# A hybrid convolution and attention block on one core: three pieces of work moved in the step order

## The chip, the cores and the metric

The kernel runs on one core of a Trainium2 chip. What counts is the device time of one execution in microseconds (us), the median of several runs. The core has five engines with a queue each: TensorE (PE: matmuls, PEld: its weight loads), VectorE (DVE), ScalarE (ACT), GpSimd (POOL) and SyncE (SP), whose queue here only issues DMAs. An engine executes its queue in order; semaphores tie the queues together.

## The reference

One layer of a diffusion block, 1024 tokens, width 1024, all in float32:

```python
h = rms_norm(x, g_pre) * (1 + sc) + sh              # sc, sh from silu(c) @ w_mod
ua, gate_a, q, k, v, gate_b, gm = split(h @ w_in)   # context tokens give k_c, v_c only
q, k = rope(rms_norm(q)), rope(rms_norm(k))         # 16 query heads, 4 key heads, 64 wide
o = softmax(q @ k_all.T / 8) @ v_all                # 1024 + 256 keys
y_attn = (o * silu(gate_b)) @ w_attn_out
a, g = split(ua); y = a * sigmoid(g)
y = depthwise_conv(y, 31 taps) + conv_b
y_conv = (silu(layer_norm(y)) * silu(gate_a)) @ w_conv_out
out = (sigmoid(ga) * y_conv + sigmoid(gb) * y_attn) @ w_out
x + gt * rms_norm(out, g_post)
```

## The kernel before, in words

Precision. A float32 operand of the large matmuls is split into a high and a low part, and three matmuls (`mm3`) replace one: high by high, low by high, high by low. Splitting a weight tile is a load (`wraw`), a cast on ACT (`whi`) and a subtraction on POOL or DVE (`wlo`).

Channels are laid on partitions, in 8 blocks of 128; tokens run along the free dimension.

**Fill steps.** All projections that no one waits for at once (convolution input, gates, sigmoids) stand in one generator, `fill`. One fill step is one `mm3` of 128x512, and 16 of them make one weight block for all tokens. There are NF = 720 of these steps ahead of the convolution's output projection. `filler(n)` issues n of them between the pieces of other work, so that PE always has something to do.

**Taps.** The depthwise convolution is 31 steps on DVE for each of the 8 channel blocks: `first` (on ACT) starts the sum, then 30 `tap`s add one shifted product of 128x1024. They stand in a list, `taps`; `pump(n)` issues the next n. Block 0 accumulates in SBUF (`acc`), blocks 1 to 7 start in PSUM in a tile `pconv` of the pool `conv`; the last tap of a block writes to SBUF. `in_psum` holds whether new sums start in PSUM, and which block is there. When `in_psum[0]` is false, the next tap moves the sum to SBUF, and the next block starts there. `last` adds the block to `ysum` on POOL and stores it to DRAM (`accD`).

**Order of the program.** (1) Preamble: modulation, normalisation and the context's keys, and then `rope_tables()` and the split weights of the first of four head groups (`group_w(0)`), both with fill steps between. (2) A loop of 4 x 4 projections: `qkv_mm` (48 matmuls of 128x384, `po`), then `per` fill steps, between which stand taps, and the steps of a generator `bg` that prepares the next group's weights. (3) The remaining fill steps up to number 464, with a tap for each two of them. Here the keys and the first rows for attention are loaded from DRAM (`load_group`, `max_load`). (4) The switch: the PSUM pools `conv` and `m`/`o` are given up, and the pools for attention opened in their place (`s` for scores, three buffers `m`). `max_piece(0, i)` finds row maxima of window 0: a matmul to `pm`, and a maximum over it on DVE (`mx`). (5) Attention: 16 windows of 20 steps (`i` in the loop over `2 * NS`). A step issues one score (two matmuls to `ps`, an exponential on ACT), one `max_piece` of the next window and one fill step; every tenth step issues 20 matmuls `po` for the values. Generators in `late` do other work at numbered steps, and their `yield n` says after how many steps they go on: `conv_rest` issues the remaining taps, the layer norm's mean (`ln_mean`: two matmuls of `ones` with `ysum`), its variance (`ln_var`), and the normalised and gated result (`z_prep`). (6) Output projections.

**What sets the order on each engine.** Up to the end of stage 2, PE, DVE, ACT and POOL keep program order. From there PE alone keeps it. A list scheduler orders the other engines, with a higher priority for what stands under `urgent()` (the maxima and exponentials, and the steps of `late`, these after the newest maximum).

In the rows below and in the trace, all operations have the line L51 (a helper), and are told apart by their tiles. A tap in PSUM is `pconv<-y,cw,pconv`, one that moves the sum is `acc<-y,cw,pconv`, and one in SBUF is `acc<-y,cw,acc`.

Of the kernel before, what the change touches and what calls it, by code (L numbers as in the profile page):

```python
# [35 lines left out]
def block_kernel(ctx: ExitStack, tc: tile.TileContext, x, cx, cc, wmod, bmodT, bmodg, vecs, gpost,  # L36
# [30 lines left out]
    def tl(tag, shape, bufs, dtype=F32, pool="sb"):  # L67
        return pools[pool].tile(list(shape), dtype, tag=tag, bufs=bufs, name=nm(tag))
# [6 lines left out]
    def closed(p):  # L75
        p.__exit__(None, None, None)
# [572 lines left out]
    def pump(n):  # L649
        for _ in range(min(n, len(taps))):  # L650
            taps.pop(0)()
# [26 lines left out]
    in_psum = [True, 0]  # L678
# [213 lines left out]
    ln = {}  # L892
# [60 lines left out]
    def z_prep():  # L953
        a, g = {}, {}

        def load(j):
            a[j] = tl("y4", (P, T), 3)
            SP.dma_start(out=a[j][:], in_=accD[j][:])
        load(0)
        for j in range(KD):  # L960
            g = tl("y4", (P, T), 3)
            SP.dma_start(out=g[:], in_=gaD[j][:])
            yield 3
            if j + 1 < KD:
                load(j + 1)
            yield 3
            for tok in HALVES:
                V.tensor_tensor(out=a[j][:, tok], in0=a[j][:, tok], in1=ln["r"][:, tok], op=ALU.mult)
                yield 1
            yield 1  # L970
            th = tl("ysum", (P, T), 1)
            S.activation(th[:], a[j][:], AF.Tanh, scale=lngh[:, j:j + 1], bias=lnbh[:, j:j + 1])
            S.activation(a[j][:], a[j][:], AF.Identity, scale=lng[:, j:j + 1], bias=lnb[:, j:j + 1])
            G.tensor_tensor(out=a[j][:], in0=a[j][:], in1=g[:], op=ALU.mult)
            yield 3
            for tok in HALVES:
                V.scalar_tensor_tensor(out=a[j][:, tok], in0=th[:, tok], scalar=1.0, in1=a[j][:, tok], op0=ALU.add,
                                       op1=ALU.mult)
                yield 1
            SP.dma_start(out=gaD[j][:], in_=a[j][:])  # L980
            yield 1

    zt = []

    def z_split(hf):
        a = {}

        def load(j):
            a[j] = tl("y4", (P, 512), 3)
            SP.dma_start(out=a[j][:], in_=gaD[j][:, hf * 512:hf * 512 + 512])  # L990
        if hf == 0:
            zt.extend(halves(KD))
        load(0)
        load(1)
        yield 3
        for j in range(KD):
            if j + 2 < KD:
                load(j + 2)
            split(zt[j][0][hf][:], zt[j][1][hf][:], a[j][:])
            yield 1 + j % 2  # L1000
# [137 lines left out]
    def filler(n):  # L1138
        done[0] += n
        return run(fill, n)  # L1140
# [3 lines left out]
    def work(n):  # L1144

        for _ in range(n):
            filler(1)
            owed[0] = min(owed[0] + RATE, 3.0)
            while owed[0] >= 1:
                pump(1)  # L1150
                owed[0] -= 1

    RATE = 0.25
    ck = ctx_kv()
    for d in ctx_h():
        work(d)
    RATE = 0.45
    for d in ck:
        work(d)
    RATE = 0.2  # L1160
    closed(stp)
    app = opened("A")
    wgp = opened("wg")
    for d in rope_tables():
        work(d)
    ones_rows()
    for d in group_w(0):
        work(d)
    prev = None
    bg = iter(())  # L1170
    per = (NF - done[0] - NB - 72) // 16
    for g in range(NG):
        for q in range(4):
            mm = qkv_mm(g, q)
            next(mm)
            if prev:
                qkv_rope(*prev)
            else:
                pump(3)
            next(mm)  # L1180
            next(mm)
            pump(3)
            next(mm)
            due = 0 if q == 3 else -1
            if q == 2 and g < NG - 1:
                bg = group_w(g + 1)
                next(bg)
            for i in range(per):
                filler(1)
                if i % 5 in (1, 3):  # L1190
                    pump(1)
                if i == 2 and prev:
                    qkv_tr(*prev)
                if i == 4:
                    z = next(mm)
                if i == 9:
                    z = qkv_scale(g, q, z)
                if i == due:
                    d = next(bg, None)
                    due = i + d if d else -1  # L1200
            if q == 3:
                run(bg)
            prev = (g, q, z)
    RATE = 0.5
    work(2)
    qkv_rope(*prev)
# [13 lines left out]
    while NF - done[0] > NB + 16:  # L1220
        filler(2)
        pump(1)
    in_psum[0] = False
    while in_psum[1]:
        pump(1)
    unshare(2)
    share({"m": 3, "o": 1})
    share({"s": 2})
    for i in range(20):
        filler(1)  # L1230
        max_piece(0, i)
        if i % 2:
            with tc.issue_after(crit[0].ins):
                pump(1)
    max_cols(0)
# [20 lines left out]
    def conv_rest():  # L1256
        while taps:
            pump(1)
            yield 2
        yield 3  # L1260
        ln_mean()
        yield 6
        yield from ln_var()
        yield from z_prep()
    later(1, conv_rest())
    for i in range(2 * NS):
# [25 lines left out]
        for g in late.pop(i, []):  # L1292
            with tc.issue_after(crit[0].ins), urgent():
                d = next(g, None)
# [81 lines left out]
```

## Time and profile before

| what | value |
|---|---|
| median of 3 runs (lowest to highest) | 1450.83 us (1448.73 to 1453.27) |
| the profiled execution: its time, its span | 1451.74 us, 1449.7 us |
| PE busy | 1384.7 us, 96% of the span |
| DVE busy | 998.6 us, 69% |
| stage 1 (to the first `po` of the projections) | 0 to 150.7 us |
| stages 2 and 3 (to the first `pm` of window 0) | to 560.9 us |
| stage 4 (to the first wait of a score) | to 586.6 us |
| stage 5 | to about 1222 us |
| stage 6 | to 1449.7 us |

The span runs from the first instruction to the last; 2.0 us of the execution lie outside it. In a row of the timeline stand the start, the duration, the engine, and `output<-inputs`; what follows in brackets is the time the engine idled before, and what ended it. In a row of windows stand, for each engine, its busy time and number of instructions, then the granted TensorE clock (1.00 is full), the DMA share and GB/s.

### The profile page before, as it was taken

Reading aid. Unit: us, or ns where it says so; the run is one execution under the profiler, and the core shown is the slowest. Engines: PE = TensorE matmul, PEld = TensorE weight load, DVE = VectorE, ACT = ScalarE, POOL = GpSimd, SP = SyncE. Lnnn points to the kernel's source line nnn. Section 1 sums busy time; section 2 is a strip of 40 time slices with the busy share of each in tenths; the row PEclk is TensorE's granted clock in tenths of the full one; section 3 lists DMA queues with packets and bytes.
Section 4 is the critical chain, followed back from the end, with each engine's and each line's share of the span. In section 5 each row is a group of like instructions: output and inputs, shape, how many; then the busy total and the mean of one; then the engine's idle time right before and its main releaser. Section 6 shows DMA issues by size and latency. Waiting matters only on the chain.

```text
span 1449.7 us, 18678 instructions
## 1 busy us (share of the span) xinstructions
PE 1384.7 (96%) x6584; PEld 1049.8 (72%) x6584; DVE 998.6 (69%) x1289; ACT 551.4 (38%) x1359; POOL 528.2 (36%) x359
## 2 busy tenths in 40 slices
PE   5988999999999998679999999999999999999998
PEld 3777989889898887446666666666666666676886
DVE  3477988888978897957776767777686653263522
ACT  5442344344443422225444444544454333031211
POOL 1124324334243210246764655565554454000000
PEclk9999999999999999889999999999999999999999
DMA  9514223224122257024553454553364223966522
GB/s 318 198 64 134 86 77 111 94 84 144 63 68 95 84 172 210 30 66 136 170 168 110 131 168 124 161 160 118 102 198 143 88 90 102 315 216 218 181 87 73
DMA packets 115898, 194.12 MB, mean 134 GB/s; under 512 B 16558, under 2 KB 46806, under 8 KB 115804
## 3 DMA queue, kind: packets, MB, share of 16 engines
q1 hardware_dynamic: 106076, 176.08, 37.4%
q10 hardware_dynamic: 9728, 16.85, 4.0%
q8 instruction: 52, 0.85, 0.3%
q14 instruction: 42, 0.34, 0.1%
HBM read 134.20 MB, written 58.55 MB: 133 GB/s over the span
## 4 chain that ended last, share of the span: by engine, by line
PE 77%; DVE 11%; DMA 5%; issue 4%; ACT 1%; POOL 1%; SPq 0%; ACTq 0%; DVEq 0%; POOLq 0%
PE ppj L51 33%; PE po L51 21%; PE ps L51 12%; PE pm L51 10%; DVE acc L51 2%; DVE pconv L51 2%; DVE mx L51 1%; DMA ogs<-ogD 1%; DVE wlo L51 1%; DVE y L51 1%; DMA r<-r1D 1%; DMA ts<-in_wout 1%; DVE ts L51 1%; DMA wm<-in_wmod 1%; DVE og L51 0%
## 5 line engine op out<-in xcount | busy, mean ns | idle before, releaser
L51 PE MATMUL ppj<-t,whi 128*128 128x512 f32 x1728 | 612.2, 398 | 9.2 <-DVE y L51 3.5
L51 PEld LDWEIGHTS ppj<-t,whi 128*128 128x128 f32 x1728 | 326.5, 189 | 95.3 <-issue 18.8
L51 PE MATMUL ppj<-t,wlo 128*128 128x512 f32 x864 | 339.0, 392 | 0.0
L51 DVE TENSOR_REDUCE mx<-pm 128x1 f32<-128x512 f32 (+1 forms) x320 | 213.9, 683 | 110.7 <-PE pm L51 107.6
L51 ACT ACTIVATE pe<-ps 128x512 f32<-128x512 f32 x320 | 190.1, 597 | 203.3 <-PE ps L51 177.3
L51 DVE SCALAR_TENSOR_TENSOR pconv<-y,cw,pconv 128x1012 f32<-128x1012 f32 (+14 forms) x190 | 243.0, 1279 | 9.3 <-ACT pconv L51 5.0
L51 PE MATMUL ps<-r,kk 128*128 128x512 f32 (+1 forms) x640 | 202.5, 398 | 11.7 <-DVE acc L51 11.1
L51 POOL TENSOR_TENSOR psum<-psum,pe 128x512 f32<-128x512 f32 x128 | 186.6, 1472 | 38.8 <-ACT pe L51 34.8
L51 PEld LDWEIGHTS ppj<-t,wlo 128*128 128x128 f32 x864 | 163.3, 189 | 29.8 <-issue 0.5
L51 PEld LDWEIGHTS ps<-r,kk 128*128 128x128 f32 (+1 forms) x640 | 120.6, 190 | 42.3 <-DVE acc L51 11.5
L51 PE MATMUL po<-pe,vt 128*64 128x512 f32 x640 | 144.4, 597 | 0.0
L51 POOL TENSOR_TENSOR wlo<-wraw,whi 128x512 fp32r<-128x512 f32 x57 | 79.4, 1406 | 163.9 <-ACT whi L51 140.4
L51 PE MATMUL pm<-kk,r 128*128 128x512 f32 (+1 forms) x384 | 127.4, 361 | 3.6 <-DVE mx L51 3.1
L51 POOL TENSOR_TENSOR psum<-psum,part 128x512 f32<-128x512 f32 x64 | 88.0, 1377 | 115.9 <-DVE part L51 115.2
L51 PE MATMUL po<-wgh,t 128*128 128x384 f32 x512 | 130.1, 335 | 0.0
L51 ACT CAST whi<-wraw 128x512 fp32r<-128x512 f32 x126 | 77.6, 633 | 83.8 <-PE ppj L51 41.0
L51 PEld LDWEIGHTS po<-pe,vt 128*64 128x64 f32 x640 | 43.1, 136 | 84.8 <-issue 84.8
L51 DVE TENSOR_TENSOR wlo<-wraw,whi 128x512 fp32r<-128x512 f32 x69 | 61.5, 892 | 57.0 <-ACT whi L51 56.7
L51 PEld LDWEIGHTS po<-wgh,t 128*128 128x128 f32 x512 | 92.9, 188 | 1.2
L51 PEld LDWEIGHTS pm<-kk,r 128*128 128x128 f32 x384 | 73.1, 191 | 21.7 <-DVE mx L51 5.0
L51 POOL TENSOR_TENSOR psum<-pe,pe 128x512 f32<-128x512 f32 x32 | 43.5, 1362 | 121.6 <-ACT pe L51 120.6
L51 PE MATMUL po<-wgl,t 128*128 128x384 f32 x256 | 85.7, 335 | 0.0
(209 smaller groups left out, 1610.1 us busy)
## 6 DMA issues: line engine op xcount, KB each, us to landing
wraw<-in_wch SPq DMA_DIRECT2D x96, 256.0 KB
wm<-in_wmod SPq DMA_DIRECT2D x16, 512.0 KB
r1D<-r1st SPq DMA_DIRECT2D x32, 256.0 KB
y<-accD SPq DMA_DIRECT2D x16, 512.0 KB
r<-r1D ACTq DMA_DIRECT2D x32, 256.0 KB
ogD<-og SPq DMA_DIRECT2D x32, 256.0 KB
ogs<-ogD SPq DMA_DIRECT2D x32, 256.0 KB
x<-in_x SPq DMA_DIRECT2D x8, 512.0 KB
```

What stands on the lines that cost most here:

```text
L51: i = f(*a, **k)
```

## The change

It has four parts.

1. The loop that moves the convolution's running sum out of PSUM stands right behind the projection loop, ahead of the last 62 fill steps of stages 2 and 3, instead of behind them (402 fill steps are done there now; it was 464).
2. In the 20 pieces of window 0's maxima, 4 taps are issued instead of 10. The taps still owed where attention begins are 13 instead of 3.
3. `rope_tables()` is not run out in the preamble, with 14 fill steps between its parts. Its two loads are issued there, and its 8 multiplications become the background work of the first projection. The 14 fill steps move behind: `per` is 21 instead of 20.
4. In attention, `ln_mean` comes 14 steps after the last tap instead of 3: at step 41, before at step 10. `ln_var` ends at step 113 (82), and `z_prep` is made shorter by 4 steps for each of the 8 blocks, so that it ends at step 201 (202).

```diff
@@ z_prep
             SP.dma_start(out=g[:], in_=gaD[j][:])
-            yield 3
+            yield 2
             if j + 1 < KD:
                 load(j + 1)
-            yield 3
+            yield 2
             for tok in HALVES:
                 V.tensor_tensor(out=a[j][:, tok], in0=a[j][:, tok], in1=ln["r"][:, tok], op=ALU.mult)
                 yield 1
-            yield 1
             th = tl("ysum", (P, T), 1)
...
             G.tensor_tensor(out=a[j][:], in0=a[j][:], in1=g[:], op=ALU.mult)
-            yield 3
+            yield 2
...
@@ before the projections
-    for d in rope_tables():
-        work(d)
+    bg = rope_tables()
+    next(bg)
     ones_rows()
     for d in group_w(0):
         work(d)
     prev = None
-    bg = iter(())
...
-            due = 0 if q == 3 else -1
+            due = 0 if q == 3 else 1 if (g, q) == (0, 0) else -1
...
-            if q == 3:
+            if q in (0, 3):
                 run(bg)
             prev = (g, q, z)
+    in_psum[0] = False
+    while in_psum[1]:
+        pump(1)
     RATE = 0.5
     work(2)
...
     while NF - done[0] > NB + 16:
         filler(2)
         pump(1)
-    in_psum[0] = False
-    while in_psum[1]:
-        pump(1)
     unshare(2)
     share({"m": 3, "o": 1})
     share({"s": 2})
     for i in range(20):
         filler(1)
         max_piece(0, i)
-        if i % 2:
+        if i % 5 == 4:
             with tc.issue_after(crit[0].ins):
                 pump(1)
@@ conv_rest
-        yield 3
+        yield 14
         ln_mean()
```

The engines' queues at three places. First POOL at the end of the preamble: `wlo` is the low part of a fill step's weights, `wgl` that of the first head group's. Before:

```order
L51 TENSOR_TENSOR wlo_1245<-wraw_1222,whi_1244 128x512
L51 TENSOR_TENSOR wlo_1264<-wraw_1224,whi_1263 128x512
L51 TENSOR_TENSOR wgl_1318<-wgr_1285,wgh_1317 128x768
L51 TENSOR_TENSOR wlo_1340<-wraw_1321,whi_1339 128x512
L51 TENSOR_TENSOR wgl_1344<-wgr_1288,wgh_1343 128x768
L51 TENSOR_TENSOR wlo_1358<-wraw_1323,whi_1357 128x512
```

Now:

```order
L51 TENSOR_TENSOR wgl_1251<-wgr_1212,wgh_1250 128x768
L51 TENSOR_TENSOR wlo_1261<-wraw_1238,whi_1260 128x512
L51 TENSOR_TENSOR wgl_1271<-wgr_1215,wgh_1270 128x768
L51 TENSOR_TENSOR wlo_1278<-wraw_1240,whi_1277 128x512
L51 TENSOR_TENSOR wgl_1294<-wgr_1218,wgh_1293 128x768
L51 TENSOR_TENSOR wgl_1311<-wgr_1221,wgh_1310 128x768
```

Before, both halves of the next fill weights (`wlo_1245`, `wlo_1264`) are split ahead of the group's first part. Now that part stands first, and the weights of the fill steps between here and the projection (`wlo_1261`, `wlo_1278`) behind its first and second part.

Then DVE at the switch of the PSUM pools, from the last maximum ahead of the first score on. Before:

```order
L51 TENSOR_REDUCE mx_5460<-pm_5502 128x1
L51 SCALAR_TENSOR_TENSOR pconv_5125<-y_922_4636,cw,pconv_5125 128x1018
L51 SCALAR_TENSOR_TENSOR pconv_5125<-y_922_4636,cw,pconv_5125 128x1019
L51 SCALAR_TENSOR_TENSOR pconv_5125<-y_922_4636,cw,pconv_5125 128x1020
L51 SCALAR_TENSOR_TENSOR pconv_5125<-y_922_4636,cw,pconv_5125 128x1021
L51 SCALAR_TENSOR_TENSOR pconv_5125<-y_922_4636,cw,pconv_5125 128x1022
L51 SCALAR_TENSOR_TENSOR pconv_5125<-y_922_4636,cw,pconv_5125 128x1023 x2
L51 SCALAR_TENSOR_TENSOR acc_5283<-y_922_4636,cw,pconv_5125 128x1022
L51 SCALAR_TENSOR_TENSOR acc_5283<-y_922_4636,cw,acc_5283 128x1021
L51 SCALAR_TENSOR_TENSOR acc_5283<-y_922_4636,cw,acc_5283 128x1020
L51 SCALAR_TENSOR_TENSOR acc_5283<-y_922_4636,cw,acc_5283 128x1019
L51 TENSOR_REDUCE mx_5460<-pm_5528 128x1
```

Now:

```order
L51 TENSOR_REDUCE mx_5448<-pm_5490 128x1
L51 SCALAR_TENSOR_TENSOR acc_5152<-y_921_4629,cw,acc_5152 128x1020
L51 TENSOR_REDUCE mx_5448<-pm_5516 128x1
L51 SCALAR_TENSOR_TENSOR acc_5152<-y_921_4629,cw,acc_5152 128x1021
L51 TENSOR_REDUCE mx_5448<-pm_5530 128x2
L51 SCALAR_TENSOR_TENSOR acc_5152<-y_921_4629,cw,acc_5152 128x1022
L51 TENSOR_REDUCE mx_5448<-pm_5544 128x1
L51 TENSOR_REDUCE mx_5448<-pm_5556 128x1
L51 SCALAR_TENSOR_TENSOR acc_5152<-y_921_4629,cw,acc_5152 128x1023
```

Seven taps of block 7 in PSUM, the tap that moves the sum and three more stood in one row here. Now the block has been in SBUF for a while, and its taps stand between maxima.

Last PE at the layer norm's mean (`pm<-ysum,ones`), in program order, with the fill step, the score and the maximum's matmul ahead of it. Before:

```order
L51 MATMUL po_5660<-pe_5618,vt_5015 64x512
L51 MATMUL ppj_5647<-t_23_124,whi_5449 128x512
L51 MATMUL ppj_5647<-t_23_124,wlo_5450 128x512
L51 MATMUL ppj_5647<-t_24_125,whi_5449 128x512
L51 MATMUL ps_5678<-r_982_5017,kk_5010 128x512
L51 MATMUL ps_5678<-r_984_5021,kk_5011 128x512
L51 MATMUL pm_5684<-kk_5010,r_987_5027 128x512
L51 MATMUL pm_5688<-ysum_733,ones 128x512
L51 MATMUL pm_5691<-ysum_733,ones 128x512
```

Now:

```order
L51 MATMUL ppj_6202<-t_21_122,whi_5964 128x512
L51 MATMUL ppj_6202<-t_21_122,wlo_5965 128x512
L51 MATMUL ppj_6202<-t_22_123,whi_5964 128x512
L51 MATMUL ps_6206<-r_1122_5664,kk_5020 128x512
L51 MATMUL ps_6206<-r_1160_5793,kk_5021 128x512
L51 MATMUL pm_6213<-kk_5020,r_1215_6006 128x256 x2
L51 MATMUL pm_6218<-ysum_733,ones 128x512
L51 MATMUL pm_6221<-ysum_733,ones 128x512
```

The pieces around it are the same, but the mean stands 31 steps later in attention: it came right behind the first 20 value matmuls (`po`), and is now at step 41. On DVE the last tap of block 7 has 26 of the steps' maxima ahead of it now (11 before).

More of the change, by code (lines that the diff above doesn't have):

```diff
@@ L981, in z_prep @@
             yield 1
+        ln["z"] = True
     zt = []
@@ L990, in load @@
             SP.dma_start(out=a[j][:], in_=gaD[j][:, hf * 512:hf * 512 + 512])
+        assert "z" in ln
         if hf == 0:
```

## The prediction

> **What bounds the kernel now.** First the page's first part.
>
> ```profile
> span 1449.7 us, 18678 instructions
> PE 1384.7 (96%) x6584; PEld 1049.8 (72%) x6584; DVE 998.6 (69%) x1289; ACT 551.4 (38%) x1359; POOL 528.2 (36%) x359
> ```
>
> PE is busy for all but 65 us of the span, and no matmul is added or removed here. So the time can change only by where PE stands idle, and by the clock it gets. The waits of PE, longest first, name the places:
>
> ```profile
> PE ps L51 <- DVE acc L51: 11.1, 1, 11.1
> PE pm L51 <- POOL ysum L51: 10.8, 1, 10.8
> PE ppj L51 <- DVE y L51: 3.5, 1, 3.5
> ```
>
> These three are single waits, and each part of the change touches one. The first two in the timeline, and four windows of 5 us behind them (PE's busy time is the number after the length, the granted clock the third from the end):
>
> ```profile
> 584.01 1.84 ACTq L51 DMA_DIRECT2D r<-mr  x2
> 586.98 9.20 DVE L51 SCALAR_TENSOR_TENSOR pconv<-y,cw,pconv 128x1018 f32<-128x1018 f32 x7
> 596.41 1.28 DVE L51 SCALAR_TENSOR_TENSOR acc<-y,cw,pconv 128x1022 f32<-128x1022 f32 x1 [0.23 <-ACT acc L51]
> 597.74 3.13 PE L51 MATMUL ps<-r,kk 128*128 128x512 f32 x6 [11.12 <-DVE acc L51]
> 618.97 7.10 DVE L51 SCALAR_TENSOR_TENSOR acc<-y,cw,acc 128x1014 f32<-128x1014 f32 x4
> 629.24 2.34 POOL L51 TENSOR_TENSOR ysum<-ysum,acc 128x1024 f32<-128x1024 f32 x1 [5.54 <-DVE acc L51]
> 631.63 3.78 PE L51 MATMUL pm<-ysum,ones 128*128 128x512 f32 x4 [10.84 <-POOL ysum L51]
> 595.00:600.00 5.00, 2.26 (x5) 1.51 (x6) 4.70 (x4) 0.90 (x3) 0.00 (x0) 0.50 0.00 0
> 600.00:605.00 5.00, 5.00 (x17) 3.98 (x17) 4.96 (x6) 1.80 (x4) 2.15 (x2) 0.67 0.00 0
> 630.00:635.00 5.00, 3.37 (x5) 1.51 (x5) 0.00 (x0) 0.60 (x1) 1.57 (x1) 0.50 0.62 213
> 635.00:640.00 5.00, 5.00 (x19) 3.89 (x18) 1.56 (x3) 1.79 (x3) 1.50 (x2) 0.76 0.00 0
> ```
>
> At 586.6 PE is at the first score, whose PSUM belongs to the convolution's pool until the tap at 596.41 has read it; DVE has kept seven PSUM taps for last, behind the urgent maxima. At 620.8 PE reaches the layer norm's mean and waits until the last taps and POOL's `ysum` are done, with all of attention queued behind. After each gap PE runs at half clock for some microseconds.
>
> **The sum out of PSUM earlier (gain 12.9).** The order of the change has no PSUM tap at the switch: the moving tap stands in DVE's queue at the end of the projections. So nothing holds the pool, and the 11.1 us go, but for what is late next: the row maxima of the score's second matmul. Their two loads are issued from 584.01 to 585.85. The nearest small load that a queue waits for is this:
>
> ```profile
> SPq L881 <- DMA recD<-rc: 18.7, 11, 4.0
> ```
>
> 1.7 us in the mean and at most 4.0, so the first of the two lands at about 586.3 and the second at 587.6; PE has a matmul of the score to do before. I put 1.0 back (0 to 2.2). The clock: 2.26 busy at 0.50 is 1.1 us lost, and 5.00 at 0.67 is 1.65. In all 11.1 - 1.0 + 2.8 = 12.9.
>
> **The mean at step 41 (gain 13.7).** The last tap stands on DVE at step 26 now. The step's length:
>
> ```profile
> 1055.14 4.44 PE po L51 x20
> 1092.90 4.44 PE po L51 x20
> 760.00:780.00 20.00, 20.00 (x114) 14.09 (x114) 7.97 (x12) 6.79 (x13) 7.50 (x6) 1.00 0.50 133
> ```
>
> 20 steps in 37.8 us, 1.89 each, so 15 steps leave 28 us for the tap's end and a `ysum` of 2.3. The 10.8 go whole. The clock behind: 3.37 busy at 0.50 (1.7) and 5.00 at 0.76 (1.2), 2.9 us. Sum 13.7.
>
> **What DVE still owes (cost 2, 0 to 7).** The taps are not saved. 19 stand in attention's first 26 steps, 49 us of PE. The window above is a stretch with neither taps nor layer norm: DVE needs 7.97 of 20 us, so 19.5 of 49. A tap costs:
>
> ```profile
> L51 DVE SCALAR_TENSOR_TENSOR acc<-y,cw,acc x43: 1260/1277/2839, 82.1 to 627.9; 128x1009 f32<-128x1009 f32 x3, 128x1010 f32<-128x1010 f32 x3, 128x1011 f32<-128x1011 f32 x3, 128x1012 f32<-128x1012 f32 x3
> L51 DVE SCALAR_TENSOR_TENSOR pconv<-y,cw,pconv x190: 1262/1279/1290, 165.3 to 594.9; 128x1023 f32<-128x1023 f32 x14, 128x1010 f32<-128x1010 f32 x13, 128x1011 f32<-128x1011 f32 x13, 128x1012 f32<-128x1012 f32 x13
> ```
>
> Minimum, median, maximum in ns: the sum in PSUM never costs over 1290, the one in SBUF up to 2839, since POOL is at work beside it. POOL is busy for 7.50 of 20 us in the window above, and the four taps at 618.97 took 1.78 each. With 1.28 DVE has 44 us of work for 49, with 1.62 (between) 50, with 2.0 58. Three `pm` buffers let PE run some 4 us ahead, so the stalls are 0, about 2 with bursts, or 7. I take 2.
>
> [...]
>
> **Denser `z_prep` (cost 2, 0 to 8).** Its second DVE step waits for POOL's product already:
>
> ```profile
> 821.28 0.63 DVE L51 TENSOR_TENSOR y<-y,acc 128x512 f32<-128x512 f32 x1
> 828.71 1.75 DVE L51 SCALAR_TENSOR_TENSOR y<-ysum,y 128x512 f32<-128x512 f32 x1 [1.06 <-POOL y L51]
> 878.17 0.68 DVE L51 TENSOR_TENSOR y<-y,acc 128x512 f32<-128x512 f32 x1
> 886.66 0.69 DVE L51 SCALAR_TENSOR_TENSOR y<-ysum,y 128x512 f32<-128x512 f32 x1 [2.20 <-POOL y L51]
> ```
>
> From the end of the first step to the product it is 6.8 and 7.8 us. In DVE's order there were 5 or more steps between, now 3: without the value matmuls (4.44 in ten steps) that is 4.4 us, and DVE waits up to 3.4. Behind it stand the maxima, for which PE waits when its three buffers are full, after some 4 us. So PE mostly gets by: a quarter of a microsecond for each of 8 blocks, 2; at 1 us each, 8.
>
> **Rope tables (cost 0.8, from a gain of 0.6 to 2.4).** The wait goes, but see what it stood before:
>
> ```profile
> 127.49 2.56 SPq L146 DMA_DIRECT2D wraw<-in_wch  x2
> 131.53 0.46 SPq L558 DMA_DIRECT2D wgr<-in_wq  x1
> 136.01 0.83 ACT L51 CAST wgh<-wgr 128x768 fp32r<-128x768 f32 x1 [9.69 <-DMA wgr<-in_wq]
> 136.91 1.98 POOL L51 TENSOR_TENSOR wgl<-wgr,wgh 128x768 fp32r<-128x768 f32 x1 [7.22 <-DMA wgr<-in_wkv]
> 138.85 1.45 POOL L51 TENSOR_TENSOR wlo<-wraw,whi 128x512 fp32r<-128x512 f32 x1
> 138.07 0.47 PE L51 MATMUL ppj<-t,whi 128*128 128x512 f32 x1 [3.50 <-DVE y L51]
> 140.00:142.00 2.00, 2.00 (x6) 1.58 (x5) 2.00 (x2) 0.00 (x0) 2.00 (x2) 0.50 0.32 74
> 146.81 4.64 POOL L51 TENSOR_TENSOR wgl<-wgr,wgh 128x768 fp32r<-128x768 f32 x2 [2.31 <-ACT wgh L51]
> 150.81 8.34 PE po L51 x48
> 159.16 13.64 PE ppj L51 x60
> ```
>
> PE stood still from 134.57 to 138.07, then ran at half clock for some time. But the 14 fill steps (0.68 each by the last row, 9.5 us) covered the first group's weights, and these now have to come sooner. Their loads stand ahead of the two `wraw` loads and are issued some 2.6 us earlier; with the same 4.5 us to land they are there at 133.4. Then POOL: 0.9 for ACT's cast, 2.0 (`wgl`), 1.5 (`wlo_1261`) make 137.8, for which PE's next fill step waits, 3.2 us. After that POOL needs 2.0 + 1.5 + 2.0 + 2.0 (2.3 for a `wgl` beside taps) to the last `wgl`, 145.3 to 146.4, and PE an eighth and a half of 8.34 more: the projection ends at 150.5 to 151.6. Before it was 159.15, or 149.6 without the 9.5. So 0.9 to 2.0 lost; with a landing 1.5 sooner, none or a small gain. POOL's chain hides any half clock. The 8 multiplications go into DVE's first projection, where it ends with the value matmuls anyway: nothing; without that cover 5 us of DVE.
>
> **The last projection (cost 1.5, 0 to 3).**
>
> ```profile
> 505.29 0.17 DVE L51 TENSOR_SCALAR stat<-stat 128x10 f32<-128x10 f32 x1
> 518.37 0.83 DVE L51 TENSOR_TENSOR qk<-qk,qkt 128x640 f32<-128x640 f32 x1
> 522.64 0.36 ACT L51 CAST kst<-pm 64x256 fp32r<-64x256 f32 x1 [0.91 <-PE pm L51]
> ```
>
> Between `stat` and the rotated queries DVE has 10 taps and a `wlo` now instead of 7 taps: 3 x 1.28 + 0.7 = 4.5 us later, where PE's transposes had 3 us in hand, and one fill step more. The rest of what is queued there (loads of keys and rows) moves back by some 7 us and had about 10.
>
> **SP at step 26 (cost 1, 0 to 4).** The eighth sum's store waits for the last tap, and behind it in SP's queue stand the first window's reciprocals and half a weight block.
>
> **Sum.** 12.9 + 13.7 - 2 - 2 - 0.8 - 1.5 - 1 = 19.3. From the profiled 1451.74 (span 1449.7 and 2.0 around it) that is 1432.4; the median of the runs is 0.9 lower: 1431.5, so 1432.
>
> **Rivals.**
> - Nothing comes back: DVE's 49 us suffice, the chains hide, and only the rope and the score's wait cost. 26.6 - 0.8 = 25.8, 1425. For it: the median tap is 1277. Against it: 7.10 us for four.
> - DVE becomes the bound in attention: the upper bounds of its two costs (7 and 8) with the other three leave 26.6 - 18.3 = 8.3, 1442. For it: DVE in the taps' steps is at 50 of 49 us. Against it: it has 28 us of steps without either work between the last tap and the mean.
> - The mean still waits: the taps end over 28 us late, and only the first wait goes, 12.9 less some 10: 1448. Against it: it takes over 3 us for each tap.
> - Slower: in `z_prep` DVE's wait for POOL's product stops PE long enough to drop its clock, 3.5 us as at 134.57 and half of 3.3 us behind, 5.1 in each of 8 blocks: 1432 + 41 = 1473. It decides once DVE's wait is about 7 us (4 of buffers and 19.3 / 8); by the rows it is 3.4.
>
> **How the numbers follow.** Forecast 0.60 (1424 to 1440 by itself), nothing back 0.14, DVE's bound 0.16, the mean still waiting 0.05, slower 0.05. Faster by over 0.3% (4.4 us, what a measurement of this kernel can tell from no change): the first three, 0.90; within it 0.05; slower 0.05. The ends by the bounds: 28 us gained, 1423, and nearly nothing gained, 1450; with 2 in 10 left out, 1423 to 1444.
>
> **What would show it.** Right: no wait of PE on `acc` or `ysum`, no window at half clock between 560 and 660, taps between the maxima, the mean some 60 us after the first score. PE waits of 2 to 4 us for `wlo` or `wgl` near 135 instead of the 3.5. Wrong: waits of PE on `mx` of over 10 us in sum between the first score and step 113, or a `pm` that waits for `ysum`.

## The result

The changed kernel takes **1438.9 us** (median of 4 runs, 1438.2 to 1441.7); the kernel before took 1449.8 beside it (1448.6 to 1453.3). The ratio is **0.9925 [0.9902, 0.9948]**: 10.9 us faster. The forecast was 1432, 18 to 19 us less, with a range from 1423 to 1444. The direction was right and so were the two main places, and some 7 us of the gain did not come.

The first part of the page of the changed kernel, and below it five rows of PE's waits, longest sum first (what is waited for, microseconds in all, times, longest). The rows left out, the longest of them 11.2 us for the first loads of modulation weights (`wm`), are within 0.6 us of what they were before:

```profile
span 1436.4 us, 18677 instructions
PE 1384.3 (96%) x6584; PEld 1051.2 (73%) x6584; DVE 999.4 (70%) x1289; ACT 550.5 (38%) x1358; POOL 533.7 (37%) x359
```

```profile
PE pm L51 <- DVE mx L51: 10.0, 8, 4.4
PE ps L51 <- ACT pe L51: 3.1, 5, 1.2
PE ppj L51 <- POOL wlo L51: 3.1, 1, 3.1
PE po L51 <- POOL wgl L51: 3.0, 2, 2.3
PE pm L51 <- DVE qk L51: 1.1, 1, 1.1
```

The span is 13.3 us shorter at the same busy time of PE. The three waits of before are gone: nothing waits for `acc` or `ysum` any more, and the 3.5 us on `y` near 135 us are gone too. In their place stand 10.0 us for the maxima (5.9 before, as the sum of six waits), 3.1 for ACT's exponentials (`pe`; 0.6 before), and in the preamble 3.1 and 3.0 for `wlo` and `wgl`.

Where PE lost time, by stretches of the two kernels (length, then PE's busy time; the granted clock is the third number from the end). The kernel before:

```profile
124.00:170.00 46.00, 42.50 (x192) 36.12 (x191) 37.55 (x35) 14.72 (x49) 21.61 (x12) 0.96 0.44 138
500.00:560.00 60.00, 57.08 (x258) 46.94 (x256) 48.78 (x56) 17.84 (x38) 9.89 (x6) 1.00 0.64 187
560.00:640.00 80.00, 55.70 (x217) 39.76 (x218) 69.24 (x79) 15.87 (x29) 18.40 (x12) 0.83 0.20 64
640.00:760.00 120.00, 116.75 (x559) 78.80 (x557) 89.82 (x113) 55.72 (x96) 80.26 (x51) 1.00 0.46 150
760.00:1200.00 440.00, 438.40 (x2109) 297.36 (x2109) 306.35 (x407) 201.60 (x348) 245.80 (x169) 1.00 0.43 133
```

The changed kernel:

```profile
124.00:170.00 46.00, 39.90 (x168) 34.27 (x167) 35.88 (x37) 13.63 (x46) 22.53 (x12) 0.89 0.44 136
500.00:560.00 60.00, 56.51 (x258) 46.60 (x257) 57.02 (x63) 17.57 (x50) 8.00 (x5) 1.00 0.46 132
560.00:640.00 80.00, 72.14 (x319) 52.11 (x318) 73.15 (x85) 21.66 (x40) 26.72 (x15) 0.96 0.35 107
640.00:760.00 120.00, 118.61 (x562) 79.90 (x561) 88.86 (x112) 53.46 (x94) 74.46 (x49) 1.00 0.43 140
760.00:1200.00 440.00, 435.74 (x2081) 294.77 (x2081) 306.22 (x409) 203.94 (x352) 258.89 (x176) 1.00 0.44 139
```

From 560 to 640 us, the stretch that the change is about, PE is busy for 72.1 instead of 55.7 us. Against that stand 2.6 us more of idle time in the preamble and 2.7 more in the attention behind 760. What half clock costs I count as PE's busy time times what is missing of the clock, in windows of 2 us. Idle and half clock together, the first four stretches lose 5.2, 2.9, 30.0 and 3.3 us before, and 10.8, 3.5, 10.7 and 1.4 after.

The two places where the changed kernel still loses most, in its timeline. The first, in the preamble (PE only):

```profile
136.04 0.50 PE L51 MATMUL ppj<-t,wlo 128*128 128x512 f32 x1 [3.09 <-POOL wlo L51]
143.75 0.45 PE L51 MATMUL po<-wgl,t 128*128 128x384 f32 x1 [2.31 <-POOL wgl L51]
146.50 0.69 PE L51 MATMUL po<-wgl,t 128*128 128x384 f32 x1 [0.70 <-POOL wgl L51]
153.46 0.39 PE L51 MATMUL ppj<-t,whi 128*128 128x512 f32 x1
```

and the window of 5 us behind the last of these waits:

```profile
145.00:150.00 5.00, 4.30 (x14) 3.79 (x13) 4.93 (x3) 1.25 (x11) 1.45 (x1) 0.50 0.62 196
```

The waits are the forecast ones (3.1, then 3.0). But the projection ends at 153.46, not at 150.5 to 151.6, because PE ran its last part at half clock behind the last wait.

The second, behind the first weighing (DVE, POOL and PE):

```profile
612.50 8.95 DVE L51 SCALAR_TENSOR_TENSOR acc<-y,cw,acc 128x1022 f32<-128x1022 f32 x4
614.33 8.24 POOL L51 TENSOR_TENSOR psum<-psum,pe 128x512 f32<-128x512 f32 x4 [0.60 <-ACT pe L51]
621.38 0.68 DVE L51 TENSOR_REDUCE mx<-pm 128x1 f32<-128x512 f32 x1
622.11 0.80 PE L51 MATMUL pm<-kk,r 128*128 128x512 f32 x1 [4.40 <-DVE mx L51]
570.84 0.79 PE L51 MATMUL pm<-kk,r 128*128 128x512 f32 x1 [2.17 <-DVE mx L51]
```

Four taps in a row take 8.95 us on DVE, 2.2 each, while POOL makes its additions of exponentials, the four in the row above at 2.1 each. The maximum stands behind the four taps, and PE, with its three `pm` buffers full, waits 4.40 us for it. The last row is an earlier wait of the same kind.

### The profile page after: what moved, and what is told of

It is laid out like the page before. It is cut to its first block, busy times and chain, and to the rows that moved or that the text cites. A ratio compares the mean times of both kernels' runs of the same rounds, so it can differ in the third digit from the quotient of the medians.

```text
span 1436.4 us, 18677 instructions
## 1 busy us (share of the span) xinstructions
PE 1384.3 (96%) x6584; PEld 1051.2 (73%) x6584; DVE 999.4 (70%) x1289; ACT 550.5 (38%) x1358; POOL 533.7 (37%) x359
## 4 chain that ended last, share of the span: by engine, by line
PE 78%; DVE 9%; DMA 5%; issue 3%; ACT 2%; POOL 2%; SPq 1%; ACTq 0%; DVEq 0%; POOLq 0%
PE ppj L51 33%; PE po L51 22%; PE ps L51 12%; PE pm L51 11%; DVE acc L51 3%; DMA ogs<-ogD 2%; DVE mx L51 1%; DVE y L51 1%; DMA wraw<-in_wch 1%; DVE ts L51 1%; DVE wlo L51 1%; DVE pconv L51 1%; DMA r<-r1D 1%; DMA wm<-in_wmod 1%; POOL wlo L51 0%
## 5 line engine op out<-in xcount | busy, mean ns | idle before, releaser
L51 DVE SCALAR_TENSOR_TENSOR pconv<-y,cw,pconv 128x1020 f32<-128x1020 f32 (+14 forms) x157 | 200.8, 1279 | 7.4 <-ACT pconv L51 3.6
L51 POOL TENSOR_TENSOR psum<-psum,pe 128x512 f32<-128x512 f32 x128 | 190.2, 1503 | 36.6 <-ACT pe L51 32.5
L51 PE MATMUL po<-wgh,t 128*128 128x384 f32 x512 | 133.4, 342 | 0.0
L51 DVE SCALAR_TENSOR_TENSOR acc<-y,cw,acc 128x1017 f32<-128x1017 f32 (+14 forms) x77 | 114.5, 1499 | 0.7
L51 PEld LDWEIGHTS pm<-kk,r 128*128 128x128 f32 x384 | 73.3, 191 | 27.5 <-DVE mx L51 10.8
```

The lines of the kernel that those rows point to most:

```text
L51: i = f(*a, **k)
```

## The experiments

Each kernel was timed beside the kernel before (whose medians were 1451.2, 1450.2 and 1451.8 us). The gain is (1 - ratio) x 1450. The five columns on the right are what PE lost in the profiled run of each, idle and half clock together, in microseconds. Two kernels, no_pool_adds and before_no_adds, leave out work that the layer needs; they are there to measure it.

| kernel | us | ratio [95%] | gain | 124-170 | 500-560 | 560-640 | 640-760 | 760-1160 |
|---|---|---|---|---|---|---|---|---|
| before | 1449.8 | 1 | 0 | 5.2 | 2.9 | 30.0 | 3.3 | 1.6 |
| changed | 1438.9 | 0.9925 [0.9902, 0.9948] | 10.9 | 10.8 | 3.5 | 10.7 | 1.4 | 3.5 |
| sum_only | 1449.1 | 0.9984 [0.9971, 0.9998] | 2.3 | 3.6 | 6.0 | 25.1 | 2.7 | 1.6 |
| mean_only | 1450.0 | 0.9991 [0.9980, 1.0003] | 1.3 | 5.2 | 4.0 | 24.4 | 2.3 | 6.9 |
| sum_mean | 1443.8 | 0.9942 [0.9927, 0.9958] | 8.4 | 4.0 | 6.4 | 11.8 | 2.2 | 7.2 |
| undo_rope | 1441.3 | 0.9924 [0.9903, 0.9945] | 11.0 | 5.1 | 4.3 | 13.3 | 0.9 | 6.2 |
| later_weights | 1434.0 | 0.9873 [0.9853, 0.9894] | 18.4 | 0.0 | 6.1 | 12.7 | 0.9 | 6.3 |
| no_pool_adds | 1430.6 | 0.9860 [0.9836, 0.9885] | 20.3 | 10.5 | 3.5 | 1.6 | 1.4 | 4.4 |
| before_no_adds | 1448.4 | 0.9977 [0.9966, 0.9987] | 3.3 | 3.9 | 3.1 | 25.9 | 6.3 | 1.6 |
| undo_taps | 1438.1 | 0.9914 [0.9890, 0.9937] | 12.5 | 8.1 | 3.5 | 8.6 | 1.6 | 5.0 |
| wlo_pool | 1436.3 | 0.9906 [0.9884, 0.9927] | 13.6 | 8.0 | 9.1 | 1.7 | 1.4 | 4.4 |
| both | 1429.1 | 0.9857 [0.9838, 0.9875] | 20.7 | 0.0 | 7.6 | 4.6 | 0.9 | 5.9 |
| both12 | 1436.4 | 0.9894 [0.9878, 0.9909] | 15.4 | 6.6 | 8.8 | 6.9 | 0.7 | 4.9 |
| both12p | 1432.0 | 0.9867 [0.9847, 0.9886] | 19.3 | 6.6 | 0.4 | 9.3 | 0.7 | 5.0 |

The profiles of kernels with the same preamble differ there by up to 3 us (changed 10.8, undo_taps 8.1), so a column difference of that size is no finding by itself.

### The two main parts alone

The prediction added a gain of 12.9 for the sum that leaves PSUM earlier and one of 13.7 for the later mean. Each was put on the kernel before by itself. The sum:

```diff
             prev = (g, q, z)
+    in_psum[0] = False
+    while in_psum[1]:
+        pump(1)
     RATE = 0.5
...
-    in_psum[0] = False
-    while in_psum[1]:
-        pump(1)
     unshare(2)
```

> The kernel before (1449.8 us) with the convolution sum moved out of PSUM at the end of the projections, and nothing else changed. Theory A, the prediction's terms stand by themselves: the wait of 11.1 us before the first score goes, the wait at the mean stays 10.8: 1437 to 1439. Theory B: both waits have one cause, DVE working through the taps from 557 to 629 us without a pause, and the mean still comes only when the last tap is done: what is won at the score is waited at the mean, whose wait grows to 18 us or more; 1446 to 1451.

```profile
PE pm L51 <- POOL ysum L51: 14.6, 1, 14.6
PE pm L51 <- DVE mx L51: 7.7, 5, 4.2
```

These are two rows of its waits of PE. Theory B holds by its time. The wait of 11.1 before the first score is gone, and the mean waits 14.6 instead of 10.8, the maxima 7.7 instead of 5.9, and the projections' end loses 3.1 more: 2.3 us are left. (The forecast wait at the mean was 18 or more; a part of it was spent earlier, at the maxima.)

The mean, with the shorter steps of `z_prep` as in the change:

```diff
-        yield 3
+        yield 14
         ln_mean()
```

> The kernel before with the mean 11 steps later and the shorter steps of z_prep, and nothing else changed. Theory A, the terms stand by themselves: the wait of 11.1 us before the first score stays, the one of 10.8 at the mean and the half clock behind it (2.9) go, and z_prep's shorter steps cost 2 to 3: 1438 to 1440. Theory B: DVE's taps still stop PE, on the maxima in place of the mean: waits on mx of 5 us or more between the first score and the mean, 1442 to 1446.

```profile
PE ps L51 <- DVE acc L51: 11.1, 1, 11.1
PE pm L51 <- DVE mx L51: 9.1, 10, 2.9
```

No wait for `ysum` is left in its list, and still only 1.3 us are won, less than either theory gave; the interval includes no gain at all. By the table, 5.6 us are won from 560 to 640 and 1.0 from 640 to 760. Of that, 5.3 go in the attention behind 760, where `z_prep` now runs, and 1.1 ahead of 560. The stretch from 560 to 640 keeps the 11.1, gets waits of 2.93 and 1.12 us for `mx` behind 620 us that were not there, and loses 8.8 to half clock (5.7 before).

Both together (the two diffs above on the kernel before), with the maxima's ten taps and the rope tables as before:

```diff
+    in_psum[0] = False
+    while in_psum[1]:
+        pump(1)
     RATE = 0.5
...
-        yield 3
+        yield 14
         ln_mean()
```

> The kernel before with the two parts together that did nothing alone (the sum out of PSUM earlier, the mean 11 steps later with z_prep's shorter steps); ten taps between the maxima and the rope tables in the preamble as before. Theory A, one backlog of taps on DVE stood behind both waits, and only both edits together let PE past it: 9 to 13 us less than before, 1437 to 1441, no wait on acc or ysum. Theory B, the other two parts (taps, rope tables) are needed as well: under 5 us, 1445 or more.

```profile
PE pm L51 <- DVE mx L51: 14.2, 13, 4.6
```

8.4 us, a little under theory A's range, and 4.8 more than the two alone add up to (by the three intervals, between 1 and 8). There is no wait on `acc` or `ysum`; PE waits 14.2 us for `mx` instead, as this row of its list shows. So the two waits of before were two views of one thing: DVE was behind with its taps, and PE met this first at the score and then at the mean. Taking one away moves the wait to the other. The interval of sum_mean overlaps that of the changed kernel, so the other two parts (the rope tables, fewer taps between the maxima) add at most little. Each is undone by itself below (undo_rope, undo_taps), and neither makes a difference that can be told from none.

### The rope tables

Undone, with everything else of the change kept:

```diff
-    bg = rope_tables()
-    next(bg)
+    for d in rope_tables():
+        work(d)
     ones_rows()
     for d in group_w(0):
         work(d)
     prev = None
+    bg = iter(())
...
-            due = 0 if q == 3 else 1 if (g, q) == (0, 0) else -1
+            due = 0 if q == 3 else -1
...
-            if q in (0, 3):
+            if q == 3:
                 run(bg)
```

> The changed kernel (1438.9 us) with the rope tables back in 14 fill steps ahead of the first group's weights. Theory A, the move of the tables is what was mis-sized: between 124 and 170 us PE lost 10.8 us (6.1 idle, 4.7 to the half clock) in the changed kernel and 5.2 before, so undoing it gains 5 to 6 us: 1433 to 1434, no wait of PE on wgl, and the old wait of about 3.5 us on y. Theory B, the prediction's own price of 0.8 us holds and the missing microseconds lie elsewhere: 1438 or more, within 1 us of the changed kernel.

```profile
124.00:170.00 46.00, 42.62 (x192) 36.19 (x191) 37.74 (x35) 15.03 (x50) 21.52 (x12) 0.96 0.47 138
...
560.00:640.00 80.00, 70.30 (x307) 50.14 (x306) 69.61 (x84) 22.13 (x40) 27.28 (x16) 0.94 0.35 112
760.00:1200.00 440.00, 432.96 (x2062) 290.73 (x2062) 305.42 (x402) 198.94 (x346) 250.11 (x172) 1.00 0.42 134
```

Three stretches of it. Theory B by the time: the ratio is 0.9924 against 0.9925. Theory A was right about the place and wrong about the whole. In the two profiles the preamble loses 5.1 us again instead of 10.8, and against these 5.7 us stand 0.8 more from 500 to 560, 2.6 more from 560 to 640 and 2.7 more behind 760. The 2.6 fit a PE that arrives sooner where DVE is behind with its taps; the 2.7 are not explained. The profiled run of undo_rope is its slowest (1442.9) and that of the changed kernel its fastest (1438.2), so this account is only as good as the two runs.

The other way round, the tables stay between the projections, and the first group's weights get back the fill steps that covered them:

```diff
         for k in range(0, KD, 2):
             load(k)
-        yield 6
+        yield 6 if g else 20
```

> The changed kernel with 20 instead of 6 fill steps between the loads of the first group's weights and their splits (the rope tables stay between the first projections; 20 fill steps per projection instead of 21). Theory A: what cost PE 10.8 us near 135 us is that the weights of the first group came 14 fill steps (9.5 us) sooner; with that cover back neither the wait on y of before nor the waits on wlo and wgl are left: 8 to 10.5 us less, 1428.5 to 1431. Theory B: PE is held there by POOL's chain whatever the order, and waits elsewhere in it: at most 4 us less, 1435 or more.

```profile
124.00:170.00 46.00, 45.96 (x219) 39.65 (x218) 38.18 (x35) 15.49 (x51) 23.25 (x13) 1.00 0.47 142
500.00:560.00 60.00, 55.61 (x240) 45.12 (x239) 56.55 (x58) 14.23 (x31) 11.37 (x6) 0.97 0.55 170
```

In the preamble PE has no gap at all, 10.7 us won. In the whole it is 7.5 by the ratios (0.9873 against 0.9925), since a part is waited for again: in the profile, which is of the slowest of its four runs (1437.9), 4.6 us between 500 and 640 and 2.8 behind 760. That lies between the two theories.

With 12 fill steps instead of 20 (both12, which also has the edit of wlo_pool below), 21 fill steps fit behind each projection as in the changed kernel:

```diff
-        yield 6
+        yield 6 if g else 12
```

> As the kernel both, with 12 instead of 20 fill steps between the loads of the first group's weights and their splits, so that 21 fill steps stand behind each projection as in the changed kernel, and not 20. Theory A: 6 fill steps (4 us) cover the weights, and with one fill step more per projection DVE gets more taps done ahead of 500 us: the preamble loses under 3 us, 500 to 560 under 6 (7.6 in both): 1427 to 1429. Theory B, the backlog on DVE decides and PE time won ahead of it is waited for behind it: within 1.5 us of both's 1429.1.

```profile
146.68 0.69 PE L51 MATMUL po<-wgl,t 128*128 128x384 f32 x1 [3.63 <-POOL wgl L51]
531.88 1.46 PE L51 MATMUL pm<-ident,qk 128*64 128x128 f32 x6 [3.67 <-DVE qk L51]
```

Both theories miss. 12 steps do not cover POOL's chain: PE waits 3.63 us for the last `wgl`. The kernel both (below), which differs only in its 20 steps here and 20 fill steps behind each projection, is 5 us faster.

### What the taps cost beside POOL

The changed kernel without POOL's additions in the first window:

```diff
         elif c == 1:
             acc_p[w, e] = tl("psum", (P, 512), 2, pool="B")
-            G.tensor_tensor(out=acc_p[w, e][:], in0=prob[n - 1, e][:], in1=x[:], op=ALU.add)
-        elif c not in (0, 3, 8):
+            if w:
+                G.tensor_tensor(out=acc_p[w, e][:], in0=prob[n - 1, e][:], in1=x[:], op=ALU.add)
+            else:
+                G.memset(acc_p[w, e][:], 1.0)
+        elif w and c not in (0, 3, 8):
             G.tensor_tensor(out=acc_p[w, e][:], in0=acc_p[w, e][:], in1=x[:], op=ALU.add)
-        if c in (4, 9):
+        if w and c in (4, 9):
```

> The changed kernel without POOL's additions of the exponentials in the first window (its denominators are then a constant; DVE, ACT and PE do the same work in the same order). In the changed kernel four taps in a row took 8.95 us beside four such additions, and PE then waited 4.40 us for mx at 622 us. Theory A, the two engines hinder each other: the four taps take 5.1 to 5.3 us, the wait at 622 us goes (under 1 us) and with it some 1.4 us of half clock: 4 to 6 us less, 1433 to 1435. Theory B, DVE simply has too much to do there: the four taps take about as long, or PE waits for mx 3 us or more all the same; within 1.5 us of 1438.9.

The group of the taps between 590 and 655 us in the changed kernel (count, then busy time in us and mean in ns):

```profile
L51 DVE SCALAR_TENSOR_TENSOR acc<-y,cw,acc 128x1020 f32<-128x1020 f32 (+14 forms) x19 | 32.9, 1731 | 0.1
```

The stretch from the score of step 0 to the last tap in the changed kernel:

```profile
594.00:650.00 56.00, 50.66 (x231) 35.50 (x231) 54.11 (x55) 21.22 (x39) 30.22 (x18) 0.97 0.16 53
```

The same group in the kernel without the additions:

```profile
L51 DVE SCALAR_TENSOR_TENSOR acc<-y,cw,acc 128x1020 f32<-128x1020 f32 (+14 forms) x19 | 25.6, 1347 | 0.1
```

The four taps of the burst in its timeline:

```profile
609.34 5.22 DVE L51 SCALAR_TENSOR_TENSOR acc<-y,cw,acc 128x1022 f32<-128x1022 f32 x4
```

And the stretch from the score of step 0 to the last tap there:

```profile
594.00:643.00 49.00, 48.75 (x231) 34.50 (x230) 44.65 (x55) 21.06 (x40) 5.92 (x4) 1.00 0.18 60
```

Theory A. DVE does the same 19 taps in the same order, and they take 25.6 us instead of 32.9; the four of the burst take 5.22 instead of 8.95. The same 231 matmuls need 49 us instead of 56, PE has no wait for `mx` in this stretch, and the whole is 9.4 us faster by the ratios, 9.1 of which the table has from 560 to 640: more than the 4 to 6 that theory A gave. What was taken away is POOL's work, not DVE's. So DVE's amount of work is not what stops PE there, but what POOL adds to its length.

Tap by tap: without the first window's additions 17 of the 19 take 1.25 to 1.28 us, and the other two (2.24 and 1.76) stand beside additions of the second window, which are still made; with them 8 take 1.26 to 1.27 and the other 11 take 1.67 to 2.37.

The same edit on the kernel before tells how much of this the change brought:

```diff
-        elif c not in (0, 3, 8):
+        elif w and c not in (0, 3, 8):
...
-        if c in (4, 9):
+        if w and c in (4, 9):
```

> The kernel before without POOL's additions of the exponentials in the first window (its denominators are then a constant). It tells how much of the 8 us that the same edit won on the changed kernel was there before. Theory A, the hindrance came with the taps that the change put beside POOL: before, only the four taps of 7.10 us and a few more ran beside it; the mean comes 2 to 4 us sooner, 1446 to 1448. Theory B, it was there all along: 7 us or more, 1443 or less.

```profile
L51 DVE SCALAR_TENSOR_TENSOR acc<-y,cw,acc 128x1021 f32<-128x1021 f32 (+12 forms) x13 | 16.5, 1273 | 0.2
```

```profile
628.39 3.55 PE L51 MATMUL pm<-ysum,ones 128*128 128x512 f32 x4 [6.29 <-POOL ysum L51]
```

The first row is the group of its taps in SBUF behind the first score, the second its PE timeline at the mean. Theory A: 3.3 us. The 13 taps take 16.5 us (20.8 with the additions), and the mean waits 6.3 instead of 10.8. So of the 9.4 us some 6 came with the change, in which 19 taps stand behind the first score.

The ten taps between the maxima, as before:

```diff
-        if i % 5 == 4:
+        if i % 2:
             with tc.issue_after(crit[0].ins):
                 pump(1)
```

> The changed kernel with ten taps between the first window's maxima, as before, instead of four. Theory A: the six taps cost 1.28 us each there and 1.5 to 2.2 beside POOL's additions later, and the burst behind the first weighing gets smaller: waits for mx after the first score fall by 3 us or more; 1433 to 1437. Theory B: DVE has nothing to spare between the maxima (18.6 of 20 us busy from 580 to 600), so six taps of 1.28 hold PE up by 5 to 8 us ahead of the first score and give back about as much later: 1438 to 1443.

```profile
619.19 0.80 PE L51 MATMUL pm<-kk,r 128*128 128x512 f32 x1 [4.40 <-DVE mx L51]
```

12.5 us, not to be told from the changed kernel, and the wait behind the first weighing is 4.40 us here too. Neither theory was tested, because the edit does little: on DVE two taps stand between the first window's maxima (as in the changed kernel), 19 behind the first score, and the four in a row are there. As I read it, the order puts taps where DVE is expected to be free, and between the maxima it is not. The kernel undoes part 2 of the change and nothing else, so part 2 brought nothing that can be told from none.

In the next kernel the burst is gone. POOL goes on making the fill weights' `wlo` until the first score, which frees DVE of ten of them; behind the first score, at 594.3 us, the taps then stand one by one between the maxima, and there are 14 of them instead of 19:

```diff
-    wl[0] = V
     bpp = opened("B")
...
+    wl[0] = V
     score(0, 0)
     score(0, 1)
```

> The changed kernel, in which POOL goes on making the fill weights' low parts (wlo) until the first score instead of until the end of the projections. POOL is idle from 515 to 595 us but for one ysum. In DVE's order the taps then stand singly between the maxima, with no four in a row. Theory A: DVE is what PE waits for from 560 to 630 us (mx 2.17, 4.40, 0.71 and 2.9 us of clock), and 8 wlo of 0.68 less on it are 5 us earlier: the wait of 4.40 goes, total 3 to 7 us less, 1432 to 1436. Theory B: a wlo on POOL takes 1.45 to 2 us instead of 0.68 and comes late for the fill steps: PE waits for wlo or ppj by as much; 1438 to 1442.

```profile
500.00:560.00 60.00, 54.04 (x233) 43.96 (x232) 55.05 (x54) 16.12 (x44) 16.27 (x10) 0.94 0.37 111
560.00:640.00 80.00, 78.34 (x361) 57.87 (x360) 75.57 (x89) 25.08 (x46) 36.44 (x24) 1.00 0.43 125
```

```profile
530.22 0.91 PE L51 MATMUL pm<-ident,qk 128*64 128x128 f32 x6 [3.76 <-DVE qk L51]
```

These are two stretches of it and a wait of PE in the first of them. Theory A holds from 560 to 640, where only 1.7 us are lost although POOL's additions are there and single taps still take up to 2.35. So single long taps are covered by the three `pm` buffers here, and the four in a row of the changed kernel were not. How much of the gain comes from the spacing, and how much from the five taps fewer, this run does not separate. But from 500 to 560 PE loses 5.6 us more: POOL's `wlo` now stands beside the taps there, and the last projection's queries come late. That leaves 2.7 us, just under theory A's range.

### Together, and the sum later out of PSUM

The edits of later_weights and wlo_pool in one kernel:

```diff
-        yield 6
+        yield 6 if g else 20
...
-    wl[0] = V
     bpp = opened("B")
...
+    wl[0] = V
     score(0, 0)
```

> The changed kernel with the 14 further fill steps ahead of the first group's splits and with POOL making wlo until the first score. If the preamble and the taps are two separate places, the gains add: with 8 to 10 from the first and 3 to 7 from the second, 1422 to 1428. If they share a cause (DVE's backlog, which the fill steps move), the sum is smaller by 3 us or more: 1429 or above.

Both has the lowest time of the kernels that compute the whole layer: **1429.1 us, 0.9857 [0.9838, 0.9875]** to before, 9.8 us better than the change by the ratios. The two edits by themselves were worth 7.5 and 2.7, 10.2 together, so they add, as far as the intervals tell. The time lies at the edge of the range that was given for a shared cause (1429 or above), because the single gains had been put too high.

Last, both12 with the sum leaving PSUM 14 fill steps later, behind the last projection's transposes, so that the taps beside POOL's `wlo` read PSUM:

```diff
-    in_psum[0] = False
-    while in_psum[1]:
-        pump(1)
     RATE = 0.5
...
+    in_psum[0] = False
+    while in_psum[1]:
+        pump(1)
     while NF - done[0] > NB + 16:
```

> As both12, with the sum leaving PSUM behind the last projection's transposes (14 fill steps later). About seven more taps then read PSUM and cost 1.28 us beside POOL's wlo instead of up to 2.3, and the rotated queries are not behind two chains of taps. Theory A: 500 to 560 loses 2 to 5 us less than in both12, and no wait on acc comes back at the score: 1424 to 1427. Theory B: POOL has little to do there, a tap costs 1.28 either way; within 1.5 us of both12.

```profile
500.00:560.00 60.00, 59.61 (x272) 49.25 (x271) 55.44 (x57) 18.78 (x53) 17.18 (x12) 1.00 0.59 166
```

```profile
605.01 0.55 PE L51 MATMUL pm<-kk,r 128*128 128x512 f32 x1 [1.93 <-DVE mx L51]
```

4 us better than both12 (0.9867 against 0.9894, with intervals that overlap a little), in theory A's direction; its 1424 to 1427 is missed, since both12 itself came out higher than expected. From 500 to 560 only 0.4 us are lost, instead of 8.8, and no wait on `acc` comes back. A part returns as waits for `mx` between 560 and 640. Its interval overlaps that of both, too. This edit together with the 20 fill steps of both was not run.

## Why the prediction came out as it did

Its sum was 19.3 us against the span of 1449.7; the span became 13.3 us shorter.

| step of the prediction | forecast | in the profile of the change |
|---|---|---|
| sum out of PSUM, mean later | +12.9, +13.7 | both waits gone; the stretch 560 to 640 gains 19.2 in all |
| what DVE still owes | -2 (0 to 7) | -7 (within the 19.2) |
| SP at step 26 | -1 | no wait of PE names it |
| rope tables | -0.8 | -5.6 in the preamble (0 by the times of undo_rope) |
| last projection | -1.5 | -0.6 |
| denser `z_prep` | -2 | -2.7 |
| not foreseen | 0 | +1.9 from 640 to 760, +1.6 ahead of 124 (1.4 of it half clock) |

- **The sum and the mean** were right as a pair and wrong as two terms. Alone they are worth 2.3 and 1.3 us, together 8.4. The prediction did read that DVE kept its taps for last and that the mean waited for the last of them, but it never asked what becomes of one wait when only the other is taken away. Since the change does both, its sum did not suffer from this. Its list of waits, "longest first", also passed over two rows of the kernel before: 11.3 us for `wm`, which the change does not touch, and 5.9 for `mx`, the wait that then grew to 10.0.
- **What DVE still owes** is the term that was mis-sized. The prediction had the parts nearly right: 19.5 us of other work (21.2 measured: 54.1 busy less 32.9 of taps) and 1.62 us a tap, "between" (1.73 measured). It compared 50 us of work with 49 of PE and took 2 of its bounds 0, 2 and 7. From the score of step 0 at 594.27 to the end of the last tap at 650.25 it was 56 us and not 49: 7, the upper bound. (That this bound was met is partly luck: 58 us of work against 49 is 9, less 4 for the buffers 5, and the prediction does not say where its 7 comes from.) The step that failed is "three `pm` buffers let PE run some 4 us ahead, so the stalls are ... about 2 with bursts". The four taps in a row are such a burst. At the measured 2.2 us each it is 9 us long; PE went on for 5.2 us after its start (612.50 to 617.71) and then waited 4.4. With 7 in place of 2 the sum gives 1437.4, and the profiled run took 1438.2. Of the 19 taps 11 took 1.67 to 2.37 us, and the other 8 no more than 1.27.
- **Rope tables.** The waits were forecast well (3.2, then up to the last `wgl` at 145.3 to 146.4; measured 3.09, and PE starts behind the last `wgl` at 146.50). What failed is "POOL's chain hides any half clock": the clock was at 0.50 from 145 to 150, behind the last wait, where nothing hides it. The 0.8 became 5.6 there (2.8 to 5.6 over the profiles of kernels with the same preamble). That it hardly shows in the whole was luck: by its times, undo_rope is no faster than the change.
- **The rivals.** "DVE becomes the bound in attention" (1442) came 3 us from the result and the forecast 7: its mechanism is what took the gain, with the 7 us of the taps in full and 2.7 of the 8 behind 760, where `z_prep` runs. "Nothing comes back" lost by the same 7 us; the mean did not wait (no `ysum` in the list), and `z_prep` never cost a gap with half clock.
- **Denser `z_prep`.** DVE's waits for POOL's product came as forecast, six of 1.87 to 3.13 us (up to 3.4 was the forecast). But of the idle time of PE behind them only 1.2 us are waits for the maxima, the path that was named (0.26 and 0.93); 1.6 are waits for ACT's exponentials (1.22 and 0.39), which the prediction does not mention. And 0.77 of the 2.7 stand at 1189 us, behind `z_prep`. That 2 and 2.7 are close is in part luck.
- **What was to be seen.** No wait on `acc` or `ysum`, taps between the maxima, 3.1 us for `wlo` near 135: seen. The mean came 86 us after the first score (at 679.0), not "some 60"; 41 steps at the prediction's own 1.89 us are 77 already. "No window at half clock between 560 and 660" was wrong: there were two short ones, behind 570.84 and 622.11, 1.4 us each. The waits on `mx` between the first score and step 113 came to 6 us (4.40, 0.71, 0.63, 0.24), under the 10 that were to show the forecast wrong.

## What to carry to other kernels

When two waits of one engine hang on the same late queue, they are one cost: removing either alone gains much less than its wait (here 2.3 and 1.3 us for waits of 11.1 and 10.8, and 8.4 together). Time won ahead of that queue may be waited for behind it, in part or in full: later_weights kept 7.5 us of the 10.7 it won in the preamble, undo_rope none that could be told. Cost a queue by its longest run of instructions with nothing urgent between them, at the price that they have beside their neighbours, and not by its sum over a stretch. And when work is taken out of a preamble, ask what it was covering: here the fill steps that went with the rope tables covered the first weights, and giving these back was the largest single gain left among the kernels that compute the whole layer.

## What was not expected of the hardware

**Taps in SBUF and POOL's work lengthen each other, and a tap that began first did not pay in 67 of 69 cases.** In the changed kernel POOL's additions take 1.5 us each behind the last tap (six in 9.06 us) and 2.06 beside the taps (four in 8.24 us). What a tap pays can be read from two rows of its timeline:

```profile
634.20 1.27 POOL L51 TENSOR_TENSOR psum<-psum,part 128x512 f32<-128x512 f32 x1 [0.69 <-DVE part L51]
634.58 1.96 DVE L51 SCALAR_TENSOR_TENSOR acc<-y,cw,acc 128x1013 f32<-128x1013 f32 x1
```

When the tap begins, the addition has 0.89 us left (634.20 + 1.27 - 634.58); the tap takes these and 1.07 us more. Over all 14 traces, each of the 210 taps in SBUF that began while a `wlo`, a `wgl`, an addition of exponentials or a `ysum` on POOL had over 0.23 us left took what was left and 1.07 to 1.09 us. Of the 69 beside which POOL began something later, 67 took 1.25 to 1.28 us, about what a tap takes with no POOL work beside it (1.25 to 1.29). And none of the 2321 taps read from PSUM took over 1.29 us, though 1612 of them had POOL at work beside them. So in these traces a tap's price depends on whether it reads its sum from SBUF and on what POOL has running when it begins.

**Half clock follows gaps, but not by their length alone.** Over all 14 profiles, between 124 and 700 us, each of the 24 gaps of PE of 3.38 us and more was followed by half clock that cost 1.4 to 3.7 us. Of the 20 shorter ones (1.93 to 3.28 us), 12 were followed by half clock too; five of 2.95 to 3.28 us were not, and behind three (2.42, 2.43 and 2.83 us) it came only after a second gap, 2.2 us later. One of the 12, of 2.17 us, is in the changed kernel, and the windows behind it read:

```profile
570.00:572.00 2.00, 1.16 (x3) 0.97 (x4) 2.00 (x5) 0.00 (x0) 0.00 (x0) 0.68 1.03 302
572.00:574.00 2.00, 2.00 (x8) 1.61 (x7) 1.80 (x4) 0.00 (x0) 0.00 (x0) 0.50 0.92 232
574.00:576.00 2.00, 2.00 (x10) 1.66 (x9) 2.00 (x4) 0.00 (x0) 0.67 (x1) 0.97 0.70 268
```

The half clock in these rows adds up to some 3.4 us (1.28, 2.00 and 0.12, from the clocks 0.68, 0.50 and 0.97). Each stretch of half clock between 124 and 700 us in the 14 traces is 3.41 us long or two to five times that, whatever the length of the gap.

Gaps of like length differ: behind the one of 3.09 us in the changed kernel the clock was halved for 3.41 us, and behind the one of 3.28 us in sum_mean it was not. What tells them apart was not tried.
